# Segment means over sorted ids: three schedule and column constants changed at the end of a streamed loop

## The chip, the cores and the metric

The kernel runs on one core of one Trainium2 chip. The time is the device time of one execution in microseconds (us), and a kernel is stated by the median of its runs. All instruction times below come from one profiled execution of the kernel before, counted from the start of its span.

## The reference

Ten million fp32 values come with ten million sorted int64 segment ids below 10000. The result is the mean of each segment.

```python
num_segments = int(segment_ids.max()) + 1
np.add.at(sums, segment_ids, data)
np.add.at(counts, segment_ids, 1)
return sums / np.maximum(counts, 1)
```

## The kernel before

**Tiling.** The values are cut into 128 stretches of D = 78125, one for each partition. Each stretch is cut into 90 rows of L = 875 values (the last has 250). Because the ids are sorted and a segment holds about 1000 values, a row usually holds no more than one border between two segments. So each row needs four things: the id at its start, the place of its border, the sum of all its values and the sum of those ahead of the border.

**The work of a row r.**
- SyncE (SP) loads the values, two rows to a tile `data_t` (tile t holds rows 2t and 2t+1; 18 buffers), and the probes `pr`, which are every 175th id. SP runs ahead of the loop.
- VectorE (DVE) finds from the probes in `first_look` which 175 ids hold the border, six rows at a time, and GpSimd (POOL) gathers those ids into `GT` by an indirect DMA (line 320).
- ScalarE (ACT) sums the gathered ids in `add_ids` (line 338 for rows under `HALVES` = 66, line 331 for the later ones). For the later rows this gives the place of the border, `KK[:, r]`, at once. `tl` is a correction that ACT adds to `KK` of row 89 alone.
- ACT sums the whole row in `total` (line 356). DVE sums the part ahead of the border in `split` (line 361), which reads `KK[:, r]`.

**The order.** The order is written out by hand: a loop over r issues the loads that are due, then `add_ids` for all rows up to `r + x_sum(row)`, then `total(r)` and `split(r)`, then everything listed in `after[r]`. `put(r, steps)` appends steps to that list, by default one step for each following row. Each engine works through its own part of this order, and semaphores hold it where data is missing.

**Blocks and columns.** Rows are weighed and put into output columns block by block: rows 0 to 61 by a table, rows 62 to 71 (`R1` to `RM`) and rows 72 to 93 (`RM` to `R2`, the last four borrowed from the next partition) by masks. A mask compares `KL`, the id of a row less the first id `sp` that the partition owns, with a range of columns: `pa` covers columns `C1` to `CA` for the rows from 62, `pb` covers `C2` to 78 for the rows from 72. POOL multiplies `pa` by the weighed sums into `xa` (line 731), and DVE adds up `xa` over the rows in two parts (line 739, after row 83). Rows 72 on come last, after split 89: DVE subtracts, adds and scans 22 rows (lines 601, 604, 607), weighs them (728), multiplies `pb` into `add` (731) and adds up over rows into `OUT[:, C2:79]` (739). Counts and reciprocals of these rows (`counts(RM, R2)`, lines 576 to 594) stand after split 86 and read all their `KK`. `finish` then stores `OUT` by four DMAs.

**The verdict.** Lines 531 to 564 count whether anything lay outside of what this scheme can hold (a row with two borders, an id outside of the columns that its block covers; the latter by `check_columns`, which compares the ids of rows 62, 71 and 72 with `C1`, `CA` and `C2`). The count goes into one integer, `badi`, written by DVE at line 564 behind split 80. `values_load` (line 823) has all five engines load it into a register. `finish` branches on it to a slow general path.

Of the kernel before, what the change touches and what calls it, by code (L numbers as in the profile page):

```python
# [35 lines left out]
HALVES = 66  # L36
# [6 lines left out]
R2 = NR + 4  # L43
RM = 72
RE = 84
C1, CA, C2 = 37, 65, 46
Q1 = 44


# [68 lines left out]
def kernel(  # L118
# [6 lines left out]
    nc = tc.nc  # L125
# [15 lines left out]
    ctx.enter_context(tc.manual_schedule())  # L141

    def x_sum(r):
        return 6 if r < HALVES else 4


    pr = cpool.tile([P, NR + 1, K], I64, name="pr")
# [257 lines left out]
    badi = cpool.tile([P, 1], I32, name="badi")  # L405
# [151 lines left out]
    def verdict():  # L557
        def s1():
            nc.scalar.activation(out=badj, in_=bad, func=ACT.Copy, accum_out=bads[:, 1:2])
            nc.tensor.matmul(out=badp, lhsT=ones, rhs=bads[:, 0:1], start=True, stop=False)  # L560
            nc.tensor.matmul(out=badp, lhsT=ones, rhs=bads[:, 1:2], start=False, stop=True)

        def s2():
            nc.vector.tensor_scalar(out=badi, in0=badp, scalar1=0.25 * NX * P, scalar2=None, op0=ALU.not_equal)

        return [s1, s2]
# [31 lines left out]
    def sums(a, b, weigh=True):  # L598
        def s1():
            c = min(b, NR)  # L600
            nc.vector.tensor_sub(out=B[:, a:c], in0=t_of(a, c), in1=A[:, a:c])  # L601

        def s2():
            nc.vector.tensor_add(out=XX[:, a:b], in0=A[:, a:b], in1=q5[:, 4, PAD + a - 1 : PAD + b - 1])  # L604

        def s3():
            nc.vector.tensor_tensor_scan(  # L607
                out=FF[:, a:b], data0=NBP[:, a:b], data1=XX[:, a:b], initial=FFP[:, a : a + 1],
                op0=ALU.mult, op1=ALU.add,
            )  # L610

        def s4():
            nc.vector.tensor_mul(out=RF[:, PAD + a : PAD + b], in0=FF[:, a:b], in1=RB[:, a:b])

        return [s1, s2, s3, s4] if weigh else [s1, s2, s3]
# [109 lines left out]
    def spread(a, b, mask, o, n, e=nc.vector):  # L725

        def s1():
            nc.vector.tensor_mul(out=RG[:, a:b], in0=FF[:, a:b], in1=RB[:, a:b])  # L728

        def s2():  # L730
            e.tensor_tensor(  # L731
                out=o, in0=mask, in1=view(RG[:, a : a + 1], [[0, n], [1, b - a]]), op=ALU.mult
            )

        return [s1, s2]
# [21 lines left out]
    after = defaultdict(list)  # L757

    def put(r, steps, every=1):
        for i, f in enumerate(steps):  # L760
            after[r + i // every].append(f)
# [17 lines left out]
    verdict_reg = []  # L779
# [31 lines left out]
    look = bounds[NG - 1] - X_LOOK - 2  # L811
# [8 lines left out]
    put(look + 1, edges_of(72, NR), 99)  # L820
    put(look + 4, single() + verdict()[:1])
    put(look + 7, verdict()[1:])
    after[look + 7].append(lambda: verdict_reg.append(nc.values_load(badi[0:1, 0:1], min_val=0, max_val=1)))
    put(RM, sums(R1, RM, False) + spread(R1, RM, pa[:, :, 0 : RM - R1], xa[:, :, 0 : RM - R1], CA - C1, nc.gpsimd)[:1])
    put(RM + 3, spread(R1, RM, pa[:, :, 0 : RM - R1], xa[:, :, 0 : RM - R1], CA - C1, nc.gpsimd)[1:])
    put(83, total_of(xa[:, 0 : C2 - C1, :], OUT[:, C1:C2])
# [11 lines left out]
    for r in range(-X_PIECE - X_DATA, NR):  # L838
        while pnext < NR and pnext <= r + ahead(pnext) + X_DATA:
            n = GROUPS[0] if pnext == 0 else PIECE  # L840
            load_probes(pnext, pnext + n)
            if pnext == 0:
                load_data(0)
                nt = 1
            pnext += n
        while nt < NT and 2 * nt <= r + X_DATA:
            load_data(nt)
            nt += 1
        if r == -X_DATA:
            nc.scalar.dma_start(  # L850
                out=snt[0 : P - 1, :],
                in_=segment_ids[D : N].rearrange("(p d) -> p d", d=D)[:, 0:1],
            )
        if r == -1:
            for f in after[r][: 5 * HEAD]:
                f()
        while r >= -1 and gs < NR and gs <= r + x_sum(gs):
            add_ids(gs)
            gs += 1
        if r == -1:  # L860
            for f in after[r][5 * HEAD :]:
                f()
        if r >= 0:
            total(r)
            split(r)
            for f in after[r]:
                f()
# [31 lines left out]
```

## Time and profile before

| | |
|---|---|
| median of 5 runs | 187.91 us (187.27 to 188.3) |
| the profiled execution | 188.03 us; its span 185.9 us, so 2.1 us lie around the span |
| DVE busy | 138.0 us, 74% of the span |
| ACT busy | 120.5 us, 65% |
| POOL busy | 100.6 us, 54% |
| DMA | 54.62 MB moved, 294 GB/s mean; 16 engines busy at nine tenths and more from slice 2 to slice 37 of 40 |
| DVE idle before split (line 361), waiting for `data_t` | 14.4 us |
| chain that ended last | DVE from 173.66 us on |

A busy share is a mean over the whole span; which engine or transfer sets the time is read stage by stage. A figure in brackets behind a line of the timeline is the idle time of the engine ahead of that instruction, and what ended it.

### The profile page before, as it was taken

The page shows a single profiled execution, that of the slowest core. Times are in us where ns is not written, and L with a number is a line of the kernel's source. Part 1 is how long each engine was busy: PE and PEld are TensorE (multiplying, and loading weights), DVE is VectorE, ACT ScalarE, POOL GpSimd, SP SyncE. Part 2 cuts the span into 40 slices and gives each one's busy share as a digit, 9 for nine tenths or more (in the row PEclk, how much of TensorE's full clock was granted, in tenths as well). Part 3 has the DMA queues.
Part 4 walks back from the last instruction along what each step waited for, and adds up shares of the span by engine and source line. Part 5 has one row for each costly group of instructions (what it writes and reads, how often), then busy time and mean ns, then how long its engine had stood idle before and what let it go on. Part 6 is the DMA issues. An engine that isn't in the chain of part 4 may idle for free. (4 is left out here: it accounts for less than half of the span.)

```text
span 185.9 us, 1472 instructions
## 1 busy us (share of the span) xinstructions
PE 2.2 (1%) x8; PEld 1.9 (1%) x8; DVE 138.0 (74%) x414; ACT 120.5 (65%) x371; POOL 100.6 (54%) x119
## 2 busy tenths in 40 slices
PE   0000000000002000000000000000000000010000
PEld 0000000000001000000000000000000000010000
DVE  7510099999189984857899999568869879868991
ACT  8002389913999196954927858197659777999910
POOL 4577786067744757075283664727447768781000
DMA  6999999999999999999999999999999999999200
GB/s 28 329 261 280 268 262 293 319 330 331 320 327 328 332 327 316 339 325 320 308 315 331 318 326 308 341 332 298 308 274 305 319 353 385 393 407 394 92 0 10
DMA packets 70612, 54.62 MB, mean 294 GB/s; under 512 B 60464, under 2 KB 61032, under 8 KB 70599
## 3 DMA queue, kind: packets, MB, share of 16 engines
q1 hardware_dynamic: 64667, 40.50, 74.4%
q0 software_dynamic: 5760, 14.01, 24.6%
q14 instruction: 13, 0.11, 0.2%
q10 hardware_dynamic: 172, 0.00, 0.1%
HBM read 56.59 MB, written 0.04 MB: 305 GB/s over the span
## 5 line engine op out<-in xcount | busy, mean ns | idle before, releaser
L320 POOL DMA_INDIRECT GT<-in_segment_ids_dram,IDX x90 | 90.9, 1010 | 64.5 <-ACT junk_t L356 24.4
L361 DVE SCALAR_TENSOR_TENSOR junk_v<-iota,q,data_t 128x875 bf16<-128x875 f32 x90 | 100.7, 1119 | 16.7 <-DMA data_t<-in_data_dram 14.4
L356 ACT ACTIVATE junk_t<-data_t 128x875 bf16<-128x875 f32 x90 | 83.8, 931 | 6.2 <-DMA data_t<-in_data_dram 5.9
L338 ACT ACTIVATE junk_a<-GT 128x175 f32<-128x175 int32 x66 | 22.1, 336 | 46.9 <-DMA GT<-in_segment_ids_dram,IDX 40.6
L356 ACT ACTIVATION_READ_ACCUMULATOR junk_t<-data_t 128x1 f32 x90 | 15.5, 172 | 0.0
L284 DVE TENSOR_REDUCE SG<-pr 128x6 f32<-128x30 int32 x15 | 2.7, 180 | 14.2 <-DMA pr<-in_segment_ids_dram 14.2
L331 ACT ACTIVATE junk_a<-GT,YY 128x175 f32<-128x175 int32 x24 | 9.9, 413 | 3.1 <-DMA GT<-in_segment_ids_dram,IDX 1.6
L338 ACT ACTIVATION_READ_ACCUMULATOR junk_a<-GT 128x1 f32 x66 | 9.4, 143 | 0.0
L345 DVE SCALAR_TENSOR_TENSOR q<-YY,G 128x6 f32<-128x6 f32 x11 | 1.7, 157 | 7.8 <-ACT junk_a L338 7.7
L361 DVE DVE_READ_ACCUMULATOR junk_v<-iota,q,data_t 128x1 f32 x90 | 7.4, 83 | 0.0
L331 ACT ACTIVATION_READ_ACCUMULATOR junk_a<-GT,YY 128x1 f32 x24 | 4.6, 190 | 0.0
L186 ACT ACTIVATE GT<-q 128x3150 int32<-128x3150 f32 x1 | 3.0, 2993 | 0.0
L300 DVE SCALAR_TENSOR_TENSOR IDX<-ST,wb 128x6 int32<-128x6 f32 (+2 forms) x16 | 2.6, 168 | 0.5
L293 DVE TENSOR_SCALAR far<-ST 128x6 f32<-128x6 f32 x15 | 2.6, 172 | 0.5
L287 DVE SCALAR_TENSOR_TENSOR ST<-pr,SG 128x6 f32<-128x6 int32 x15 | 2.5, 166 | 0.5
L296 DVE TENSOR_TENSOR ST<-ST,far 128x6 f32<-128x6 f32 x15 | 2.5, 166 | 0.5
L721 POOL TENSOR_SCALAR pb<-pb 128x396 f32<-128x396 f32 (+1 forms) x2 | 2.4, 1185 | 0.2
L242 DVE CAST jj<-jj_i 128x128 f32<-128x128 int32 x1 | 1.5, 1506 | 0.7 <-POOL jj_i L241 0.7
L560 PE MATMUL misc<-bads,ones 128*128 128x1 f32 x2 | 0.6, 362 | 103.1 <-ACT badj L552 103.1
L186 ACT ACT_TABLE_LOAD x1 | 1.3, 1283 | 0.7 <-PEq L883 0.7
L304 DVE SCALAR_TENSOR_TENSOR YY<-ST,SG 128x6 f32<-128x6 f32 x11 | 1.7, 158 | 0.0
L720 POOL TENSOR_TENSOR pb<-KL,jj 128x396 f32<-128x396 f32 (+1 forms) x2 | 1.6, 810 | 0.2
(126 smaller groups left out, 45.6 us busy)
## 6 DMA issues: line engine op xcount, KB each, us to landing
data_t<-in_data_dram SPq DMA_DIRECT2D x44, 875.0 KB, 10.2
GT<-in_segment_ids_dram,IDX POOLq DMA_INDIRECT x90, 6.4
pr<-in_segment_ids_dram SPq DMA_DIRECT2D x41, 10.0 KB, 7.3
data_t<-in_data_dram SPq DMA_DIRECT2D x1, 437.5 KB, 18.3
data_t<-in_data_dram SPq DMA_DIRECT2D x1, 125.0 KB
out_dram<-OUT SPq DMA_DIRECT2D x1, 36.6 KB
pr<-in_segment_ids_dram SPq DMA_DIRECT2D x1, 31.0 KB, 3.9
snt<-in_segment_ids_dram ACTq DMA_DIRECT2D x1, 1.0 KB
```

Source lines behind the costliest of these rows:

```text
L186: nc.scalar.activation(out=gt32[:, :, 0 : 2 * W : 2], in_=view(q5[:, 0, 0:1], [[0, RING], [0, W]]), func=ACT.Copy)
L284: v.tensor_reduce(out=SG[:, a:b], in_=pr32[:, a:b, 0 : 2 * K : 2], axis=AX.X, op=ALU.add)
L287: v.scalar_tensor_tensor(out=ST[:, a:b], in0=VI[:, a + 1 : b + 1], scalar=float(K), in1=SG[:, a:b], op0=ALU.mult, op1=ALU.subtract,)
L293: v.tensor_scalar(out=far, in0=ST[:, a:b], scalar1=0.0, scalar2=FAR, op0=ALU.is_equal, op1=ALU.mult)
L296: v.tensor_add(out=ST[:, a:b], in0=ST[:, a:b], in1=far)
L300: v.scalar_tensor_tensor(out=IDX[:, c:d], in0=ST[:, c:d], scalar=float(w), in1=wb[:, c:d], op0=ALU.mult, op1=ALU.add)
L320: nc.gpsimd.indirect_dma_start(out=GT[:, r % RING, :], out_offset=None, in_=ids2d[:], in_offset=bass.IndirectOffsetOnAxis(ap=IDX[:, r : r ...
L331: nc.scalar.activation(out=junk_a, in_=gt32[:, r % RING, 0 : 2 * W : 2], func=ACT.Identity, scale=-1.0, bias=YY[:, r : r + 1], accum_out=K ...
L338: nc.scalar.activation(out=junk_a, in_=gt32[:, r % RING, 0 : 2 * W : 2], func=ACT.Copy, accum_out=g_of(r, r + 1),)
L356: nc.scalar.activation(out=junk_t[:, 0:n], in_=d, func=ACT.Copy, accum_out=t)
L361: nc.vector.scalar_tensor_tensor(out=junk_v[:, 0:n], in0=iota[:, 0:n], scalar=KK[:, r : r + 1], in1=d, op0=ALU.is_lt, op1=ALU.mult, accum_ ...
L721: e.tensor_scalar(out=o, in0=o, scalar1=0.0, scalar2=None, op0=ALU.is_equal)
```

## The change

The ids of rows 66 to 89 are summed three rows ahead of the loop instead of four. So on ACT each of these sums stands behind one more `total`.

The load of the verdict into registers moves from the end of `after[80]` to the start of `after[81]`. On DVE it stood between the write of `badi` and split 81; it now stands between split 81 and split 82. On ACT it stood behind total 80 and now stands behind total 81.

Three column limits change: `C1` from 37 to 41, `CA` from 65 to 64, `C2` from 46 to 50. The mask `pa` and its product `xa` narrow from 28 to 23 columns, `pb` and `add` from 33 to 29, and the second part of the sum over `xa` from 19 to 14 columns of 11 values. The two table sums of line 696 keep their 33 and 35 columns in all and are cut at other places.

```diff
-C1, CA, C2 = 37, 65, 46
+C1, CA, C2 = 41, 64, 50
...
     def x_sum(r):
-        return 6 if r < HALVES else 4
+        return 6 if r < HALVES else 3
...
     put(look + 4, single() + verdict()[:1])
     put(look + 7, verdict()[1:])
-    after[look + 7].append(lambda: verdict_reg.append(nc.values_load(badi[0:1, 0:1], min_val=0, max_val=1)))
+    after[look + 8].insert(0, lambda: verdict_reg.append(nc.values_load(badi[0:1, 0:1], min_val=0, max_val=1)))
```

Here `look` is 73.

## The prediction

> **What bounds the kernel now.** First the slices of the span, for what is full and when. Columns are fortieths of the span (4.65 us each), digits tenths.
>
> ```profile
> DVE  7510099999189984857899999568869879868991
> ACT  8002389913999196954927858197659777999910
> DMA  6999999999999999999999999999999999999200
> GB/s 28 329 261 280 268 262 293 319 330 331 320 327 328 332 327 316 339 325 320 308 315 331 318 326 308 341 332 298 308 274 305 319 353 385 393 407 394 92 0 10
> ```
>
> The transfers fill their engines from slice 2 to 37 (to about 172 us). DVE has gaps until then, 14.4 us of them waiting for values. So the stream sets the pace until it ends, and time saved on DVE ahead of its last wait for values comes back as a longer wait. The timeline near the end says where that last wait is. Counting back from the 250-element split (row 89), these are splits 80, 81, 82 and 84 with what stands between:
>
> ```profile
> 165.12 1.13 DVE L361 SCALAR_TENSOR_TENSOR junk_v<-iota,q,data_t 128x875 bf16<-128x875 f32 x1 [0.70 <-DMA data_t<-in_data_dram]
> 166.17 0.15 DVE L564 TENSOR_SCALAR badi<-misc 128x1 int32<-128x1 f32 x1
> ...
> 167.06 1.13 DVE L361 SCALAR_TENSOR_TENSOR junk_v<-iota,q,data_t 128x875 bf16<-128x875 f32 x1 [0.74 <-ACT junk_t L356]
> ...
> 168.29 1.13 DVE L361 SCALAR_TENSOR_TENSOR junk_v<-iota,q,data_t 128x875 bf16<-128x875 f32 x1
> ...
> 170.58 0.25 DVE L739 TENSOR_REDUCE OUT<-xa 128x9 f32<-128x99 f32 x1
> ...
> 171.19 1.13 DVE L361 SCALAR_TENSOR_TENSOR junk_v<-iota,q,data_t 128x875 bf16<-128x875 f32 x1 [0.36 <-DMA data_t<-in_data_dram]
> ...
> 172.25 0.37 DVE L739 TENSOR_REDUCE add<-xa 128x19 f32<-128x209 f32 x1
> ```
>
> Splits 80 and 84 visibly wait for their tiles. The 0.74 us ahead of split 81 is put down to ACT, but that `total` had long been done; the view of line 823 shows the load of the verdict in exactly this gap. Split 82 shows no wait, but the trace's completion records, put on this clock by splits 80 and 84, have the last piece of tiles 40 to 44 at 165.06, 168.23, 171.14, 173.26 and 174.66 us. Tile 41 landed 0.06 us before split 82 started: that split is bound by the stream too, and the stall ahead of it was free. From 171.19 on no tile is late (split 86 starts 0.49 us after tile 43), and DVE runs without a gap to the stores:
>
> ```profile
> 172.77 0.29 ACT L336 ACTIVATE q<-q,tl 128x1 f32<-128x1 f32 x1
> ...
> 174.80 0.18 DVE L576 TENSOR_TENSOR ps<-q,QQ 128x22 f32<-128x22 f32 x1
> ...
> 178.95 0.18 DVE L601 TENSOR_TENSOR q<-T,q 128x18 f32<-128x18 f32 x1
> ...
> 179.89 0.92 DVE L731 TENSOR_TENSOR add<-pb,RG 128x726 f32<-128x726 f32 x1
> 180.84 0.94 DVE L739 TENSOR_REDUCE OUT<-add 128x33 f32<-128x759 f32 x1
> 181.82 1.49 SPq L745 DMA_DIRECT2D out_dram<-OUT  x2
> ```
>
> So two stages matter: up to 171.19 the stream, then 10.6 us of DVE.
>
> **Narrower columns.** Three instructions stand in that DVE stretch. Line 739 on `xa` falls from 19x11 = 209 to 14x11 = 154 elements; 99 elements took 0.252 and 209 took 0.368, so 1.05 ns each: 55 x 1.05 = 0.06 us. Line 731 falls from 33x22 = 726 to 29x22 = 638; 280 elements of the same operation took 0.441 (line 718) and 726 took 0.917, so 1.07 ns each: 88 x 1.07 = 0.09. The last line 739 falls from 759 to 667 elements: from 209 to 759 it costs 1.05 ns each, so 92 x 1.05 = 0.10. Sum 0.25 us, all on the path.
>
> The rest of the narrowing lies beside other work. The mask `pa` on DVE (143.37 us, 0.44 to 0.39) precedes split 68, which waits 0.43 for values. On POOL the first `pb` mask ends 1.67 us before the next gather may go, the product into `xa` ends at 168.12 and is read at 170.58, the second `pb` mask ends at 167.41 and is read at 179.89, and the smaller memsets at the start are followed by 2.02 us of idle time. The same number of table columns is summed as before. Without these covers they would still be gains, at most 0.05 us each on DVE and 0.1 to 0.2 on POOL.
>
> The Trainium skill says in "Perfetto Trace Analysis" (Optimizing Scalar/DVE Operations) that GpSimd and DVE share an SBUF read port, which would let less POOL work speed up DVE. Here split 80 took 1.13 us with POOL's mask work beside it and split 83 took 1.13 with POOL at rest. The sum stays at 0.25.
>
> **The verdict load.** It takes about half a microsecond in each engine's queue:
>
> ```profile
> L823 POOLq TENSOR_LOAD <-badi x1: 498/498/498, 166.4 to 166.4; - x1
> L823 DVEq TENSOR_LOAD <-badi x1: 542/542/542, 166.4 to 166.4; - x1
> ```
>
> and the timeline of POOL at that time:
>
> ```profile
> 166.35 1.06 POOL L721 TENSOR_SCALAR pb<-pb 128x330 f32<-128x330 f32 x1
> 167.37 0.75 POOL L731 TENSOR_TENSOR xa<-pa,RG 128x280 f32<-128x280 f32 x1
> ```
>
> POOL's queue did the load while line 721 ran, and line 731 followed without a gap; DVE's stood idle because the load was next in line behind the write it waits for. Behind split 81 the write is long done, and 0.54 us fit under 1.13 us of split. So split 81 starts about 0.70 us earlier, at 166.36, and split 82 could start at 167.59 (a split with its read takes 1.23). Tile 41 lands at 168.23, so split 82 starts at 168.29 as before; 83, line 739 and split 84 stand where they stood. Worth: 0. Bounds: if the load stalled DVE just as long in its new place, 167.59 + 0.74 = 168.33, a loss of 0.04; a gain needs an earlier stream (below). Behind the load on DVE is queued split 82 and nothing that another engine wants soon. On ACT the load no longer holds up sum 85 (0.38 us idle there), off the path. SP, POOL and PE wait for `badi` alone and have nothing behind the load but the stores and the branch.
>
> The skill's "DMA: Bandwidth & Descriptors" (Latency and other measured facts) gives a floor of about 600 ns for such a load. The rows show 0.48 to 0.54 us. Either fits under the split, and the sum is the same by both.
>
> **Ids three rows ahead.** No instruction is added. On ACT, sum r + 4 and `total(r)` trade places, so a `total` no longer stands behind a sum that waits for its gather (1.6 us at row 62, 1.2 us at row 74). Nobody on the path waits for those totals, and the loads do not either: tiles 31 and later are in buffers that are not filled again. Gathers 84 to 89 reuse the slots of rows 66 to 71, summed before 145 us, and start from 157.27. So the stream is as before.
>
> What moves nearer to the end is `KK` of row 89, which `counts` needs at 174.80. Before it was ready at 173.06. Now sum 89 stands behind `total(85)`. Steps from ACT's rows: a total and the next sum start 0.87 apart (171.33, 172.20), a sum and the next total 0.43, sum 89 and its correction 0.57, correction and the next total 0.20. From `total(84)` at tile 42 (171.19): sum 88 at 172.06, total 85 at 172.49, sum 89 at 173.36, correction 173.93 to 174.22. DVE now asks at 174.74, so 0.5 us are spare; if ACT starts `total(84)` only at 171.33 as before, 0.4. The last total would be read at about 177.7, asked for at 178.89. Cost 0; gather 89 lands at 171.98 and gets more room (1.4 us instead of 0.2). Splits read their `KK` three rows after it is made, some 4 us.
>
> **Sum.** 0 + 0 + 0.25: the span goes from 185.9 to 185.65 and the profiled execution from 188.03 to 187.78 us. That execution lies 0.12 over the median of the runs, so the median goes to 187.66, rounded 187.65. This is 0.13%, and about 0.3% (0.56 us) is what a measurement of this kernel can tell from no change.
>
> **Rivals.**
>
> *The stall counts after all (faster).* Before, DVE was ready for split 84 at 170.83 and waited to 171.14. If tiles 41 and 42 come more than 0.31 us earlier after tile 40 than here, the old order is held up by its stall and the new one is not; each further 0.1 us is a gain of 0.1, up to 0.70. That would give 187.65 - 0.70 = 186.95. For it: tiles 42 and 43 landed 2.12 us apart, DVE needs about 2.5 for a pair of rows. Against: 40, 41 and 42 landed 3.17 and 2.91 apart, with the last gathers among them.
>
> *The late ids take over (slower).* If ACT is a whole row (0.87 + 0.43 = 1.30 us) behind its tile at `total(84)`, the correction ends at 175.52 and `counts` waits 0.78 us from 174.74. Less the 0.25 that is 0.53 worse: 188.45. It decides from a lateness of 0.5 us, eats the saving at 0.75, and is measurable from 1.3. For it: ACT was fully busy from 160 to 173 us. Against: the wait of 1.16 and the 0.38 of the load leave its path, so it should meet tiles 41 and 42 waiting.
>
> *The narrower limits fail and the slow path runs.* On the drawn ids row 62 starts at least 47 columns into its partition (41 needed), row 72 at least 56 (50), row 71 at most 60 (63 allowed). Excluded.
>
> *The stream ends elsewhere.* The runs of before differ by 1.03 us with one order of work. A median can move by 0.25 either way.
>
> **How the numbers follow.** Tail alone, 0.60 (own range 187.35 to 188.0: the saving of 0.25 with the median's movement and some of the stall); stall counts by 0.3 or more, 0.27 (186.9 to 187.35); late ids by a row or more, 0.08 (188.45 up); a later stream, 0.05 (188.2 up). The range 186.9 to 188.2 takes in the first two and part of the last. Faster by over 0.3% (under 187.35): 0.27 and a little of the first, 0.30. Slower by over 0.3% (over 188.47): most of the last two, 0.11. Within: 0.59.
>
> **What would show it.** Split 81 right behind `badi`, and split 82 with a recorded wait of some 0.6 us for values; lines 739, 731 and 739 at about 0.31, 0.82 and 0.85 us; the correction of row 89 ending near 174.2 and line 576 right behind split 86. A wait of line 576 on ACT would make the second rival right; a split 84 without a wait before, and one after, the first. A stretch from split 84 to the stores other than 10.6 - 0.25 = 10.4 us would make the sum wrong.

## The result and the profile after

The changed kernel took 188.11 us (median of 42 runs, 187.02 to 190.9), the kernel before beside it on the same chips 187.98 us (79 runs, 186.68 to 190.49). The ratio is 1.0009 with a 95% interval of 0.9992 to 1.0025: no change that can be measured. (The ratios leave out runs more than 1.5% above the fastest of their kernel, and they are not the quotient of the medians.) The forecast was 187.65 with 0.59 on "within 0.3%". But the sum behind it said -0.25 us, a ratio of 0.9987, and that lies just below the interval. The experiments had to find what gave the quarter of a microsecond back.

The profiled execution happens to be a fast one: 186.81 us, its span 184.7. The splits 80, 81, 82 and 84 of the timeline, with what stands between (start, length, engine, line; in brackets the idle time ahead and what ended it):

```profile
164.19 1.13 DVE L361 SCALAR_TENSOR_TENSOR junk_v<-iota,q,data_t 128x875 bf16<-128x875 f32 x1 [0.73 <-DMA data_t<-in_data_dram]
...
165.24 0.15 DVE L564 TENSOR_SCALAR badi<-misc 128x1 int32<-128x1 f32 x1
165.43 1.13 DVE L361 SCALAR_TENSOR_TENSOR junk_v<-iota,q,data_t 128x875 bf16<-128x875 f32 x1
...
167.43 1.13 DVE L361 SCALAR_TENSOR_TENSOR junk_v<-iota,q,data_t 128x875 bf16<-128x875 f32 x1 [0.86 <-DMA data_t<-in_data_dram]
...
170.21 1.13 DVE L361 SCALAR_TENSOR_TENSOR junk_v<-iota,q,data_t 128x875 bf16<-128x875 f32 x1 [0.23 <-ACT junk_a L331]
...
171.26 0.31 DVE L739 TENSOR_REDUCE add<-xa 128x14 f32<-128x154 f32 x1
```

The 0.74 us between the write of `badi` and split 81 are gone, and the whole of it has come back as a wait of split 82 for its values (0.86). The wait ahead of split 84 is put down to ACT, whose sum had long been done; by the completion records, put on this clock by split 80 as in the prediction, tile 42 landed at 170.15, 0.06 us ahead of the split. The end of the timeline:

```profile
172.93 0.29 ACT L336 ACTIVATE q<-q,tl 128x1 f32<-128x1 f32 x1
...
173.76 0.18 DVE L576 TENSOR_TENSOR ps<-q,QQ 128x22 f32<-128x22 f32 x1
...
178.85 0.82 DVE L731 TENSOR_TENSOR add<-pb,RG 128x638 f32<-128x638 f32 x1
179.71 0.85 DVE L739 TENSOR_REDUCE OUT<-add 128x29 f32<-128x667 f32 x1
180.59 1.07 SPq L745 DMA_DIRECT2D out_dram<-OUT  x1
```

From split 84 to the stores: 180.59 - 170.21 = 10.38 us, against 181.82 - 171.19 = 10.63 before. The tail is shorter by exactly the forecast 0.25. So what gave it back can only lie ahead of split 84, in the stream, or in the scatter of the runs. One profile of each cannot tell: the runs of one kernel differ by several microseconds, and this profile's stream was an early one. Only many runs can.

### The profile page after: what moved, and what is told of

It reads as the page before. It is cut to its first block, busy times and chain, and to the rows that moved or that the text cites. A ratio compares the mean times of both kernels' runs of the same rounds, so it can differ in the third digit from the quotient of the medians.

```text
span 184.7 us, 1471 instructions
## 1 busy us (share of the span) xinstructions
PE 2.2 (1%) x8; PEld 1.9 (1%) x8; DVE 137.1 (74%) x414; ACT 120.6 (65%) x371; POOL 99.4 (54%) x119
## 5 line engine op out<-in xcount | busy, mean ns | idle before, releaser
L721 POOL TENSOR_SCALAR pb<-pb 128x348 f32<-128x348 f32 (+1 forms) x2 | 2.1, 1028 | 0.2
L560 PEld LDWEIGHTS misc<-bads,ones 128*128 128x128 f32 x2 | 0.5, 313 | 101.4 <-ACT badj L552 101.4
L720 POOL TENSOR_TENSOR pb<-KL,jj 128x348 f32<-128x348 f32 (+1 forms) x2 | 1.5, 733 | 0.2
```

The costliest lines, as they stand in the source:

```text
L721: e.tensor_scalar(out=o, in0=o, scalar1=0.0, scalar2=None, op0=ALU.is_equal)
```

## The experiments

Each kernel of the experiments was timed beside the kernel before on one chip. "Tail" is the time from split 84 to the stores in its profile.

| kernel | buffers | tail, us | ratio to before | 95% interval |
|---|---|---|---|---|
| changed kernel | moved | 10.38 | 1.0009 | 0.9992 to 1.0025 |
| ids alone | as before | 10.61 | 1.0005 | 0.9962 to 1.0049 |
| verdict load alone | as before | 10.63 | 0.9979 | 0.9951 to 1.0007 |
| columns alone | moved | 10.37 | 1.0031 | 1.0002 to 1.0059 |
| columns alone, again | moved | 10.37 | 1.0019 | 0.9985 to 1.0053 |
| columns, buffers put back | as before | 10.37 | 0.9966 | 0.9929 to 1.0003 |
| before, buffers moved | moved | 10.63 | 1.0021 | 0.9986 to 1.0057 |
| before, buffers moved, again | moved | 10.63 | 1.0057 | 1.0021 to 1.0092 |
| changed, buffers put back | as before | 10.38 | 0.9955 | 0.9923 to 0.9988 |
| wide columns | elsewhere | 11.79 | 1.0052 | 1.0017 to 1.0087 |
| tight columns, sums earlier | elsewhere | 10.07 | 0.9964 | 0.9931 to 0.9996 |
| late ids | moved | 11.93 | 1.0067 | 1.0036 to 1.0099 |
| load in the tail | moved | 11.12 | 1.0044 | 1.0003 to 1.0085 |

The column "buffers" was added when the first results were in; it is explained at "The addresses". The theory is that of the prediction: the stream sets split 84, DVE sets the tail.

**The three parts alone.** The ids:

```diff
-        return 6 if r < HALVES else 4
+        return 6 if r < HALVES else 3
```

> The ids of rows 66 on summed three rows ahead; columns and verdict load as in the kernel before. Tail theory (the stream sets split 84, then DVE sets the rest): no difference, 0.0 us, with 10.6 us from split 84 to the stores and the correction of row 89 ending some 0.5 us before line 576 asks for it. Rival (the late ids cost what the narrow columns save): 0.3 to 0.4 us slower, to be seen as a wait of line 576 for ACT or as a later tile 42.

1.0005, tail 10.61. In this profile the correction of row 89 ended at 173.91 and line 576 started at 174.44: 0.53 us to spare, as worked out. No cost is seen. The interval is wide enough to hold the rival's 0.3 to 0.4 us, but line 576 did not wait, which that rival needs.

The verdict load, moved alone to the start of `after[look + 8]`:

> Only the move of the verdict load. Tail theory: no difference; split 81 follows the write of badi at once, split 82 waits some 0.6 us for tile 41, and 10.63 us from split 84 to the stores. Rival (the stall counted): 0.3 to 0.7 us faster.

```profile
163.86 1.13 DVE L361 SCALAR_TENSOR_TENSOR junk_v<-iota,q,data_t 128x875 bf16<-128x875 f32 x1 [0.74 <-DMA data_t<-in_data_dram]
...
165.11 1.13 DVE L361 SCALAR_TENSOR_TENSOR junk_v<-iota,q,data_t 128x875 bf16<-128x875 f32 x1
166.91 1.13 DVE L361 SCALAR_TENSOR_TENSOR junk_v<-iota,q,data_t 128x875 bf16<-128x875 f32 x1 [0.66 <-DMA data_t<-in_data_dram]
```

These are splits 80 to 82. The stall became a wait for values of 0.66 us, as forecast. The ratio of 0.9979 does not exclude a gain up to 0.5%; the profile shows none.

The column limits alone:

```diff
-C1, CA, C2 = 37, 65, 46
+C1, CA, C2 = 41, 64, 50
```

> Only the three column limits of the change. Tail theory: 0.25 us faster than before (ratio 0.9987); from split 84 to the stores 10.38 us instead of 10.63. Rival (the columns move the stream, by the shorter work of POOL): no gain or a loss, with tile 42 landing later than in the kernel before by more than its runs differ.

The tail came out at 10.37, as summed, and the time at 1.0031, on the other side of 1; its interval does not reach the 0.9987 of the sum. This is the part in which the gain is lost.

**The tail counts one to one.** Wider columns in the changed kernel:

```diff
-C1, CA, C2 = 41, 64, 50
+C1, CA, C2 = 25, 65, 26
```

> The changed kernel with wider columns: C1, CA, C2 = 25, 65, 26, so pb has 53 columns instead of 29 and the second sum over xa 39 instead of 14. Tail theory: the tail grows by (528 + 552 elements) x 1.05 to 1.07 ns + 275 x 1.05 = 1.43 us against the changed kernel, 1.18 us against the kernel before (ratio 1.0063); from split 84 to the stores 11.8 us. If the tail were covered by something else: less than half of that.

```profile
173.32 0.60 DVE L739 TENSOR_REDUCE add<-xa 128x39 f32<-128x429 f32 x1
...
181.19 1.37 DVE L731 TENSOR_TENSOR add<-pb,RG 128x1166 f32<-128x1166 f32 x1
182.60 1.42 DVE L739 TENSOR_REDUCE OUT<-add 128x53 f32<-128x1219 f32 x1
```

The three lines of the sum grew to 0.60, 1.37 and 1.42 us, the tail to 11.79, and the time by 0.52% [0.17, 0.87]; 0.63% was expected. The interval alone would still hold half of what was expected; but the profile shows all of it in the tail, and the late ids below (a tail 1.30 us longer than before, a ratio of 1.0067 where 1.0069 was to come) say the same. Time added to the tail arrives at the end. The saving of 0.25 did not go missing there.

Tighter limits, and both sums over `xa` one row earlier:

```diff
-C1, CA, C2 = 41, 64, 50
+C1, CA, C2 = 47, 61, 56
...
-    put(83, total_of(xa[:, 0 : C2 - C1, :], OUT[:, C1:C2])
+    put(82, total_of(xa[:, 0 : C2 - C1, :], OUT[:, C1:C2])
```

> The changed kernel with the narrowest limits that these ids allow (C1, CA, C2 = 47, 61, 56: pb 23 columns, second sum over xa 5 columns), and both sums over xa a row earlier, so that the second stands ahead of split 84 and in its wait. Tail theory: from 10.38 less 0.23 (a sum that leaves the tail), less 6 x 22 x 1.07 ns = 0.14, less 6 x 23 x 1.05 ns = 0.14, so 9.87 us from split 84 to the stores; against the kernel before 0.76 us less, ratio 0.9960. If the stream only moved the end, not the tail: no difference from the changed kernel.

0.9964, with a tail of 10.07 where 9.87 was expected. The two wide lines fell to 0.69 and 0.70 us as worked out. The error is the sum that left the tail: splits 84 and 85 start 1.24 us apart without it and 1.28 with it, so it was worth 0.04 to 0.05, not 0.23. Most of such a small instruction lies in the gap that stands between two splits anyway.

**The two waits, made to bind.** Two further sums of row 85 on ACT ahead of the id sum of row 89:

```diff
-            add_ids(gs)
+            [total(r - 1) for _ in range(2 * (gs == NR - 1))]; add_ids(gs)
```

> The changed kernel, where ACT sums row 85 two times more ahead of the id sum of row 89 (2 x 1.02 us). By the prediction's slower rival with its threshold: the correction of row 89 ends 2.04 us later than 173.22, at 175.26 on the clock of the changed kernel's profile, line 576 asks for it at 173.70 and waits about 1.55 us, and the time grows by that: 1.3 us over the kernel before (ratio 1.007), with 11.9 us from split 84 to the stores. If ACT were covered further than worked out: no wait and no difference.

```profile
175.78 0.29 ACT L336 ACTIVATE q<-q,tl 128x1 f32<-128x1 f32 x1
...
176.11 0.18 DVE L576 TENSOR_TENSOR ps<-q,QQ 128x22 f32<-128x22 f32 x1 [1.46 <-ACT q L336]
```

DVE waited 1.46 us for the correction; the tail is 11.93 and the ratio 1.0067. So 2.04 us of lateness cost 11.93 - 10.38 = 1.55 us of tail: the first half microsecond was free, as the slower rival's threshold said.

The write of `badi` and the load both behind split 85, next to each other as in the kernel before:

```diff
-    put(look + 7, verdict()[1:])
-    after[look + 8].insert(0, lambda: verdict_reg.append(nc.values_load(badi[0:1, 0:1], min_val=0, max_val=1)))
+    put(85, verdict()[1:])
+    after[85].append(lambda: verdict_reg.append(nc.values_load(badi[0:1, 0:1], min_val=0, max_val=1)))
```

> The changed kernel with the write of badi and the load of the verdict both behind split 85, in the form of the kernel before (load next in line behind the write), so that the stall stands in the tail where nothing of the stream covers it. Tail theory: from split 84 to the stores 10.38 + 0.74 + 0.19 (the write's own place) = 11.3 us, 0.9 us over the changed kernel. If the stall is always covered: 10.4 to 10.6.

```profile
171.34 1.13 DVE L361 SCALAR_TENSOR_TENSOR junk_v<-iota,q,data_t 128x875 bf16<-128x875 f32 x1 [0.30 <-DMA data_t<-in_data_dram]
...
173.67 0.15 DVE L564 TENSOR_SCALAR badi<-misc 128x1 int32<-128x1 f32 x1
...
174.59 1.13 DVE L361 SCALAR_TENSOR_TENSOR junk_v<-iota,q,data_t 128x875 bf16<-128x875 f32 x1 [0.77 <-DVE badi L564]
...
182.46 1.49 SPq L745 DMA_DIRECT2D out_dram<-OUT  x2
```

The tail is 11.12 = 10.38 + 0.74. The same stall that cost nothing ahead of split 81 costs all of itself ahead of split 86. (The write's own 0.15 us, expected on top, fitted into the gap between splits.)

**The addresses.** Narrower columns change one thing that is no instruction: `pa`, `xa`, `pb` and `add` are allocated ahead of the value buffers and shrink by 55 + 55 + 88 + 92 = 290 fp32 values for each partition, so all that is allocated behind them moves down. Each tile takes a multiple of 32 bytes, so the move is 224 + 224 + 352 + 352 = 1152 bytes. First the columns alone once more, and the columns with an unused tile that puts the buffers back:

```diff
-    nc.vector.memset(RF, 0.0)
+    cpool.tile([P, 288], FP32, name="pad"); nc.vector.memset(RF, 0.0)
```

> The columns alone a second time, because the first time they came out at 1.0031 [1.0002, 1.0059] where their own instructions are 0.25 us shorter. Tail theory (the stream's own scatter did that): a ratio near 0.9987 within its interval, and 10.37 us from split 84 to the stores again. Rival (the narrower tiles move the value buffers down by 1152 bytes in SBUF, and the stream is slower there): 1.003 again.

> The columns alone, with an unused tile of 1152 bytes, so that the value buffers and all that lies behind them keep the addresses of the kernel before. Tail theory: the same as without it, 0.9987, and 10.37 us from split 84 to the stores. Address rival: 0.9987 here while the columns without the tile stay near 1.003.

1.0019 moved, 0.9966 put back, with a tail of 10.37 in both. Neither interval settles it alone: both still hold the 0.9987 of the sum. Then the reverse, no edit of the change and only the buffers moved, and the changed kernel with them put back by the same unused tile:

```diff
-    pa = cpool.tile([P, CA - C1, RM - R1 + 1], FP32, name="pa")
+    pa = gpool.tile([P, CA - C1, RM - R1 + 1], FP32, name="pa")
...
-    nc.vector.memset(RF, 0.0)
+    cpool.tile([P, 24], FP32, name="pad"); nc.vector.memset(RF, 0.0)
```

> The kernel before in every instruction, with the value buffers and the buffers of the gathered ids moved down by 1152 bytes in SBUF to where the changed kernel has them (the mask pa is allocated behind them instead, and 96 unused bytes stand ahead of them). Tail theory without addresses: no difference, and 10.63 us from split 84 to the stores. Address theory (the kernels whose buffers lie there came out 0.3 to 0.8 us above their instruction sum): 0.3 to 0.6 us slower, ratio 1.002 to 1.003, from a later split 84 and the same tail.

> The changed kernel with an unused tile of 1152 bytes, so that the value buffers lie where the kernel before has them. Tail theory without addresses: as the changed kernel, 1.001 within the interval. Address theory: the saving of the prediction comes out, 0.25 us, ratio 0.9987 or less; 10.38 us from split 84 to the stores in both.

> The kernel before with only its buffers moved down by 1152 bytes, a second time, since the first (1.0021 [0.9986, 1.0057]) tells neither theory. Address theory, with the size that the unused tile made in the two pairs (columns alone, changed kernel: about 0.65 us): 0.4 to 0.7 us slower, ratio 1.002 to 1.004. No address effect: 1.000, and the mean of both then below 1.0015.

The kernel before with moved buffers: 1.0021 [0.9986, 1.0057] and 1.0057 [1.0021, 1.0092]. Their mean is 1.0039, which is 0.7 us for no instruction at all, though the first of the two alone shows nothing (medians 188.04 moved and 188.05 before). The changed kernel with the buffers put back: 0.9955 [0.9923, 0.9988], clear of 1, where it is at 1.0009 [0.9992, 1.0025] without the tile. Its profile and that of the changed kernel have the same tail, 10.38:

```profile
172.72 1.13 DVE L361 SCALAR_TENSOR_TENSOR junk_v<-iota,q,data_t 128x875 bf16<-128x875 f32 x1
...
183.10 1.49 SPq L745 DMA_DIRECT2D out_dram<-OUT  x2
```

(This profile is of a late stream, split 84 at 172.72 against 170.21, though its runs are the faster ones: one more sign that a single profile says nothing on the stream's mean.)

Three comparisons that differ only in the place of the buffers say the same. With the intervals put together as independent: the mean of the two runs of the columns less the run with the tile, 0.59% (plus or minus 0.43); the changed kernel less the one with the tile, 0.54% (0.37); the kernel before, mean of two, 0.39% (0.25). Each interval excludes zero. The plain means of the same fast runs give smaller sizes with the same sign, and also exclude zero: 0.71 us (plus or minus 0.43), 0.56 (0.40) and 0.61 (0.43), which is 0.3 to 0.4%.

Two things keep the size uncertain. By the recorded ratios the kernels with buffers put back come out below their own sum (0.9966 for 0.9986, 0.9955 for 0.9987), which the place cannot explain, since theirs is that of the kernel before; their intervals just hold the sum. And the late ids, whose buffers are moved, show no loss beyond their tail (1.0067 [1.0036, 1.0099] for 1.0069); their interval still holds 0.3%.

What stays open: which of the moved tiles matters, why, and which addresses are good ones. All three comparisons move the value buffers, the gathered ids and the eight small tiles of the verdict (`bad` to `badj`); other tiles move in some of them only, or the other way. The tail does not change with the place, so the time is lost ahead of split 84; in which stretch, single profiles cannot show.

## Why the prediction was right, and where its sum was wrong

**The number: right, in part by luck.** 188.11 lies in the stated range of 186.9 to 188.2, and "within 0.3%" was the likeliest outcome. But the forecast gain of 0.25 us did not arrive, and 188.11 lies between the branches' own ranges: "tail alone" ends at 188.0 and "a later stream" begins at 188.2. The range held because a term that the sum lacked was about as large as the saving.

**What bounds the kernel: right.** In eleven profiles the completion records of tiles 40 and 42 can be put on the clock by a wait of split 80. In ten of them tile 42 landed 0.05 to 0.06 us before split 84 started, whatever stood ahead; the eleventh, 0.09, is taken up under the rivals. And the tail added up to what its lines cost to about 0.03 us, in all but two kernels: there a small instruction between two splits was priced at 0.23 and 0.19 us and cost 0.04 to 0.05 and nothing.

**Narrower columns, the three lines: right.** Forecast 0.31, 0.82 and 0.85 us; they took 0.31, 0.82 and 0.85. Less work on POOL did not shorten the splits: 1.13 us as before.

**Narrower columns, "the rest of the narrowing lies beside other work", and, under the ids, "so the stream is as before": this step was wrong.** As to instructions it held. But it looked for the cost of smaller tiles only in the instructions that work on them, and had no term for the places of the tiles behind them. The whole change needs this term to be 0.17 + 0.25 = 0.42 us (0.10 to 0.72, from the interval of 1.0009) if nothing else gained; the three comparisons give 0.7 to 1.1 us by the recorded ratios and about 0.6 by the plain means, with intervals that hold 0.5 us. So its sign is shown, and its size only roughly. It took back about the 0.25 of the tail.

**Verdict load: right in its profile.** Split 81 followed the write at once and split 82 took the whole stall as a wait. It started 0.77 us later than the 1.23 us after split 81 that the prediction allows it, where 0.70 was forecast (168.29 less 167.59); tile 41 landed 0.07 later after tile 40 here. The bracket's 0.86 counts from the end of split 81's own row. On DVE the load ran from 165.5 for 0.54 us, while split 81 ran from 165.43 to 166.56:

```profile
L823 DVEq TENSOR_LOAD <-badi x1: 544/544/544, 165.5 to 165.5; - x1
L823 POOLq TENSOR_LOAD <-badi x1: 492/492/492, 165.5 to 165.5; - x1
```

The floor of about 600 ns in the Trainium skill ("DMA: Bandwidth & Descriptors", Latency and other measured facts) was undercut in every profile here (0.48 to 0.55 us). Whether the move gains something in runs with closer tiles is not settled: alone it is at 0.9979 [0.9951, 1.0007], and the changed kernel with its buffers put back is at -0.45%, where the columns explain -0.13%, though its interval reaches to -0.12%.

**Ids three rows ahead: right.** With split 84 0.98 us earlier than in the profile before, the correction should have ended at 173.24 and line 576 started at 173.76; they did so at 173.22 and 173.76.

**Rivals.** The slow path did not run. The late ids have the threshold that was worked out but were not late. The fourth, "the stream ends elsewhere", was named without a mechanism and with 0.05, from 188.2 up; it is the nearest to what happened, though the median stayed below its 188.2.

The faster rival (a stall that counts) shows at its edge in one profile, the columns alone, again, where the load still stands right behind the write:

```profile
167.95 1.13 DVE L361 SCALAR_TENSOR_TENSOR junk_v<-iota,q,data_t 128x875 bf16<-128x875 f32 x1 [0.74 <-DVE badi L564]
...
169.18 1.13 DVE L361 SCALAR_TENSOR_TENSOR junk_v<-iota,q,data_t 128x875 bf16<-128x875 f32 x1
...
170.42 1.13 DVE L361 SCALAR_TENSOR_TENSOR junk_v<-iota,q,data_t 128x875 bf16<-128x875 f32 x1
...
171.47 0.25 DVE L739 TENSOR_REDUCE OUT<-xa 128x9 f32<-128x99 f32 x1
171.65 1.13 DVE L361 SCALAR_TENSOR_TENSOR junk_v<-iota,q,data_t 128x875 bf16<-128x875 f32 x1
```

Split 84 (171.65) shows no wait. Tile 42 landed 5.62 us after tile 40 here, 6.08 in the profile before, and split 84 started 0.03 us later after it than in the other profiles. So DVE set split 84, and the stall counted, for 0.03 us. The rows also correct the rival's threshold: split 84 can start 0.18 us after line 739 does, which is 170.76 in the profile before and not 170.83, so the tiles must come 0.43 us closer, not 0.31, before the stall costs anything. What it costs in the runs without a profile is not known.

## What to carry to other kernels

In a kernel bound by a stream and then by a short tail, sum the tail's lines and ignore what is saved ahead of the last wait: for the tail of this change that was right to 0.01 us. A small instruction between two long ones is the exception: a whole one of 0.31 us was worth 0.04 here. A change of a tile's size also moves every tile allocated behind it. Before a gain or loss of half a per cent is put down to instructions, time the kernel also with an unused tile that puts the addresses back. And where the runs differ by more than the effect, read from the profile only what is the same in all of them, such as the tail, and leave the rest to many timed runs.

The changed kernel with the unused tile, 0.9955 [0.9923, 0.9988], beats both kernels. The tight columns with earlier sums do so too, 0.9964 [0.9931, 0.9996], with buffers in a third place; the two were not put together.

## What the runs showed of the hardware that was not expected

The place of buffers in SBUF, with 1152 bytes between two allocations that share every instruction, made about 0.4% of the time in the kernel before (0.7 us by the ratios, 0.6 by the plain means; 0.14 to 0.64% by the interval). A register load of one integer held DVE up by 0.74 to 0.77 us when it was next behind the write that it waits for. With a split of 1.13 us between, its 0.54 us ran beside that split.
